# One pool for projections and scan, values moved forward, and a stepwise substitution in an RWKV-7 layer

## The chip, the core and the metric

The kernel runs on one core of a Trainium2 chip. The metric is device time of one execution in microseconds; before the change the median of three runs is 2736.81 us (2734.67 to 2741.68). A core has five engines that matter here: TensorE (PE in the views), VectorE (DVE), ScalarE (ACT), GpSimd (POOL) and SyncE (SP, which issues nearly all transfers). Each has its own instruction order and waits on semaphores of others. DMA moves data between HBM and the core's SBUF.

## The reference, cut to what matters

The reference is a trunk of two layers on 256 tokens with 2048 features. Layer 0 mixes by sparse attention, layer 1 by RWKV-7; each is followed by a squared-ReLU MLP, and all parts are scaled and shifted by products of silu(c). The change touches layer 1's mixer, and in passing the place where silu(c) is made:

```
delta = h_prev - h
xr, xw, xk, xv, xa, xg = (h + delta * mu[i] for i in range(6))
r, k, v = xr @ w_r, xk @ w_k, xv @ w_v
decay = exp(-exp(-softplus(-(w0 + tanh(xw @ w_w1) @ w_w2)) - 0.5))
a = sigmoid(a0 + (xa @ w_a1) @ w_a2)
g = sigmoid(xg @ w_g1) @ w_g2
def step(state, inp):                       # 32 heads of 64, 256 tokens
    sa = einsum('bhij,bhj->bhi', state, -kk_t)
    state = state * w_t + sa * (kk_t * a_t) + v_t * k_t
    return state, einsum('bhij,bhj->bhi', state, r_t)
o = layer_norm(o) * gn_g + gn_b + sum(r * k * r_k) * v
return (o * g) @ w_o
```

## The kernel before, in words

Features lie on the partitions: 16 tiles of 128 features (two heads each) by 256 tokens. All of a weight's products are made with three matmuls in reduced form (`acc3`, L181 to L186: high part of the weight with high and low part of the data, low part with high): a weight comes as four pieces of 128x512, ACT casts the high part (L92) and DVE or POOL subtracts to get the low part (L94). `bufs["g"]` says which of the four pieces' subtractions POOL does.

Layer 1's mixer runs in `rwkv_project` and `rwkv_scan`. The projections go through two loops over the 16 tiles. The first makes r (W_r) and the mixed inputs; xv, the input of the values, is kept. The second, called the W_k loop here, multiplies W_k for tile f and then makes with `elements` all that is elementwise for tile f - 1: the decayed forms of r, k, kk and a, written by ACT to DRAM as `hd`.

The scan turns the recurrence into chunks of 64 tokens, four of them. For each tile `prepare` reads `hd`, makes the value (48 dense matmuls with W_v), the within-chunk matrices `at` (L969), transposes (L975, L980) and a product with v (L994). `inverse` makes the inverses of unit triangular 64x64 matrices: first of the 32x32 diagonal blocks by doubling, four levels of 16 products (L1025) and 16 products (L1032) of 32x32 in each tile, with a masked copy, a transpose by DVE and a copy by ACT between them; then one step from 32 to 64 (L1045, L1052). `chain` then goes through the four chunks one after another: the state's part (L1080), the sum (L1082), the solve (L1085), a copy (L1086), the output (L1088) and the new state (L1099 and after). `finish` normalizes, and `out_group` multiplies with W_o from tile 5 on.

The order on each engine follows a scheduler that takes instructions by priority as their inputs and buffers come free; `high_priority(URGENT)` lets `chain` and `inverse` go ahead of the rest. Three tiles are prepared ahead (AHEAD), two inverses (AHEAD_INV). Projections and scan have SBUF pools of their own, one after the other, beside a third, `keep`, for what lives in both.

## Time and profile before

| | |
|---|---|
| median of three runs | 2736.81 us (2734.67 to 2741.68) |
| profiled execution | 2733.74 us, of which the span is 2732.0 us |
| mean granted clock of TensorE | 0.968 |
| PE busy | 2582.7 us (95%), 21876 matmuls |
| DVE busy | 1863.9 us (68%) |
| ACT busy | 1353.5 us (50%) |
| POOL busy | 1356.4 us (50%) |
| W_k loop | 1342 to 1498 us of the span |
| hand-over to the scan | 1498 to 1567 us |
| scan to the last chain | 1567 to 1947 us |

The span is the time from the first to the last instruction of the profiled execution; the profile is of that one, and the median is over other executions. A matmul of this kernel in full float32 has two records in the trace. Groups in a timeline (xcount) have a start and the time to the end of the last of the group; busy times of neighbouring matmuls overlap, since matmuls are pipelined. The clock column is a share of full speed: TensorE's two levels are 1.2 and 2.4 GHz, and a stretch at the lower one shows as 0.5.

### The profile page before, as it was taken

The page shows a single profiled execution, that of the slowest core. Times are in us where ns is not written, and L with a number is a line of the kernel's source. Part 1 is how long each engine was busy: PE and PEld are TensorE (multiplying, and loading weights), DVE is VectorE, ACT ScalarE, POOL GpSimd, SP SyncE. Part 2 cuts the span into 40 slices and gives each one's busy share as a digit, 9 for nine tenths or more (in the row PEclk, how much of TensorE's full clock was granted, in tenths as well). Part 3 has the DMA queues.
Part 4 walks back from the last instruction along what each step waited for, and adds up shares of the span by engine and source line. Part 5 has one row for each costly group of instructions (what it writes and reads, how often), then busy time and mean ns, then how long its engine had stood idle before and what let it go on. Part 6 is the DMA issues. An engine that isn't in the chain of part 4 may idle for free. (4 is left out here: it accounts for less than half of the span.)

```text
span 2732.0 us, 58247 instructions
## 1 busy us (share of the span) xinstructions
PE 2582.7 (95%) x21876; PEld 2277.7 (83%) x21876; DVE 1863.9 (68%) x2986; ACT 1353.5 (50%) x2964; POOL 1356.4 (50%) x1121
## 2 busy tenths in 40 slices
PE   6898998999999999989889899999789999999997
PEld 3566778988989989879889788888689898898996
DVE  3266568999999999769877557666797244353443
ACT  3334335555554545556555334443445565564553
POOL 1343227568577675755566212232655444444454
PEclk9899999999999999999999889999899999999999
DMA  9997745989999999736476423232486655555553
GB/s 364 402 357 261 266 149 197 322 310 374 322 334 355 324 349 337 267 110 194 141 247 213 157 78 102 93 111 97 168 314 203 212 182 189 192 182 192 186 185 104
DMA packets 263595, 624.33 MB, mean 229 GB/s; under 512 B 29328, under 2 KB 43024, under 8 KB 238352
## 3 DMA queue, kind: packets, MB, share of 16 engines
q1 hardware_dynamic: 256400, 608.03, 64.0%
q10 hardware_dynamic: 6912, 12.59, 1.3%
q8 instruction: 171, 2.80, 0.4%
q14 instruction: 112, 0.92, 0.1%
HBM read 603.72 MB, written 16.78 MB: 227 GB/s over the span
## 5 line engine op out<-in xcount | busy, mean ns | idle before, releaser
L94 POOL TENSOR_TENSOR wlo<-raw,whi 128x512 fp32r<-128x512 f32 x364 | 569.0, 1572 | 535.5 <-ACT whi L92 415.2
L92 ACT CAST whi<-raw 128x512 fp32r<-128x512 f32 x856 | 516.7, 618 | 385.7 <-PE ps_d L185 112.3
L94 DVE TENSOR_TENSOR wlo<-raw,whi 128x512 fp32r<-128x512 f32 x492 | 471.1, 969 | 207.6 <-ACT whi L92 200.1
L94 POOL TENSOR_TENSOR wlo<-more,whi 128x512 fp32r<-128x512 f32 x181 | 278.4, 1541 | 289.9 <-ACT whi L92 209.2
L92 ACT CAST whi<-more 128x512 fp32r<-128x512 f32 x366 | 223.0, 618 | 193.8 <-PE ps_m L418 44.0
L256 DVE CUSTOM_DVE_ANT_0 araw<-araw,cb 128x2048 f32<-128x2048 f32 x112 | 292.2, 2609 | 0.0
L94 DVE TENSOR_TENSOR wlo<-more,whi 128x512 fp32r<-128x512 f32 (+1 forms) x185 | 183.9, 996 | 116.9 <-ACT whi L92 116.3
L184 PE MATMUL ps_d<-A,whi 128*128 128x256 f32 x656 | 195.0, 299 | 12.2 <-ACT B L911 6.9
L185 PE MATMUL ps_d<-A,whi 128*128 128x256 f32 x656 | 189.6, 290 | 4.3 <-DVE A L198 4.2
L186 PE MATMUL ps_d<-A,wlo 128*128 128x256 f32 x656 | 188.4, 288 | 0.3 <-DVE wlo L94 0.3
L401 DVE TENSOR_TENSOR A<-B,A 128x256 fp32r<-128x256 f32 x96 | 101.9, 1061 | 96.1 <-ACT A L400 95.8
L185 PE MATMUL ps_d<-h,whi 128*128 128x258 f32 x560 | 160.7, 287 | 6.1 <-DVE h L377 6.0
L184 PE MATMUL ps_d<-h,whi 128*128 128x258 f32 x560 | 160.4, 286 | 0.0
L186 PE MATMUL ps_d<-h,wlo 128*128 128x258 f32 x560 | 159.2, 284 | 0.0
L184 PE MATMUL ps_m<-h,whi 128*128 128x258 f32 x532 | 151.3, 284 | 0.0
L185 PE MATMUL ps_m<-h,whi 128*128 128x258 f32 x532 | 150.9, 284 | 0.0
L184 PEld LDWEIGHTS ps_d<-A,whi 128*128 128x128 f32 x656 | 127.7, 195 | 27.2 <-ACT B L911 7.7
L186 PE MATMUL ps_m<-h,wlo 128*128 128x258 f32 x532 | 150.0, 282 | 0.0
L397 ACT ACTIVATE B<-B,sm 128x256 f32<-128x256 f32 x128 | 65.1, 508 | 170.6 <-DVE B L396 170.6
L185 PEld LDWEIGHTS ps_d<-A,whi 128*128 128x128 f32 x656 | 127.7, 195 | 8.0 <-DVE A L198 6.8
L186 PEld LDWEIGHTS ps_d<-A,wlo 128*128 128x128 f32 x656 | 127.8, 195 | 1.0 <-issue 0.5
L94 POOL TENSOR_TENSOR xlo<-more,xhi 128x512 fp32r<-128x512 f32 x51 | 103.6, 2031 | 45.5 <-ACT xhi L92 43.9
(545 smaller groups left out, 8200.6 us busy)
## 6 DMA issues: line engine op xcount, KB each, us to landing
araw<-ada_w_in SPq DMA_DIRECT2D x192, 1024.0 KB, 7.1
raw<-mlp_w_in SPq DMA_DIRECT2D x614, 256.0 KB, 4.1
more<-mlp_w_in SPq DMA_DIRECT2D x410, 256.0 KB, 4.5
raw<-b_w_r_in SPq DMA_DIRECT2D x64, 256.0 KB, 3.1
raw<-b_w_k_in SPq DMA_DIRECT2D x64, 256.0 KB, 3.5
raw<-b_w_v_in SPq DMA_DIRECT2D x64, 256.0 KB, 3.6
raw<-b_w_o_in SPq DMA_DIRECT2D x64, 256.0 KB, 3.3
hd<-A ACTq DMA_DIRECT2D x48, 256.0 KB, 4.0
```

Of the source, the lines that this page charges most:

```text
L92: t.nc.scalar.copy(hi[:, :n], r)
L94: e.tensor_tensor(lo[:, :n], r, hi[:, :n].bitcast(F32), op=OP.subtract)
L184: mm(out, wh, m[:, :w], start=i == 0, stop=False)
L185: mm(out, wh, m[:, w:], start=False, stop=False)
L186: mm(out, wl, m[:, :w], start=False, stop=i == n - 1)
L256: nc.vector.tensor_tensor_reduce(out=w, in0=w, in1=s.cb, scale=1.0, scalar=0.0, op0=OP.mult, op1=OP.add, accum_out=acc[:, k:k + 1])
L397: nc.scalar.activation(r, u, AF.Relu, bias=c)
L401: nc.vector.tensor_tensor(t[:, S:], q, t[:, :S].bitcast(F32), op=OP.subtract)
```

## The change

One pool "rwkv" serves projections and scan, and the ring "h" of 16 tiles, free after the projections' inputs are mixed, is used for what lives long (`H`). `value` writes its result to DRAM (`vd`); twelve of the sixteen values are made in the W_k loop, four between the first pair's steps. `within` makes the part of `at` that the inverse needs already in the W_k loop and writes it to DRAM (`nd`). `blocks` inverts all 32x32 blocks of half of the tiles at once on DVE, one matrix on each partition, by 30 steps of a product and a sum, and writes them to DRAM (`xd`): the first half of the tiles in the W_k loop, the second in the scan. `inverse` reads its blocks from there and keeps only the step from 32 to 64. `prepare_pair` and `chain` work on two tiles at a time, with copies and sums of double width. silu(c) is made once, written to DRAM (`cd`) and read where it was made again before. The sums of squares end in three tiles in place of two. (The core of the diff; line numbers in the fences below that are of the changed code differ from those of the code above.)

```diff
-AHEAD, AHEAD_INV = 3, 2
+LAG_N = 3
+LATE_V = 4
+STEPS = 4, 5
...
+    def H(s):
+
+        return s.tp.tile([P, S + 1], F32, name="h", bufs=NF)[:, :S]
...
+        if s.cd is not None:
+            nc.sync.dma_start(s.cb, s.cd[0].partition_broadcast(P))
+            return
+        s.cd = s.dram.tile([1, D], F32, name="cd")
         nc.sync.dma_start(s.cb, s.io["c"].partition_broadcast(P))
         sg = s.tp.tile([P, D], F32, name="araw", bufs=s.bufs["m"])
         nc.scalar.activation(sg, s.cb, AF.Sigmoid)
         nc.vector.tensor_tensor(s.cb, s.cb, sg, op=OP.mult)
+        nc.sync.dma_start(s.cd, s.cb[0:1, :])
...
+        s.bufs["g"] = (1, 2)
+        made, vs, sub = {}, list(range(NF - LATE_V)), None
+        for f in range(NF + LAG_N):
             if f < NF:
                 w = s.wload(io["b_w_k"][f])
                 pk = s.dense(w, xm, cols)
-            if f:
-                s.elements(f - 1, pp, omka, wa0)
-            if f == NF:
-                s.vs[0] = s.value(0, keep.tile([P, S], F32, name="v0"))
+            if 0 < f <= NF:
+                made[f - 1] = s.elements(f - 1, pp, omka, wa0)
+            if vs and (f % 3 or f >= NF):
+                s.value(vs.pop(0), s.H())
+            if f >= LAG_N:
+                s.within(f - LAG_N, *made.pop(f - LAG_N))
+            if f == NF // 2 + LAG_N - 1:
+                sub = s.blocks(0)
+            elif sub:
+                for _ in range(STEPS[0]):
+                    next(sub, None)
             pp = pk
+        assert not vs
+        for _ in sub:
+            pass
+
+    def value(s, f, v, after=None):
+        w = s.wload(s.io["b_w_v"][f])
+        p = s.dense(w, s.xv, [i * P for i in range(16)])
+        if after is not None:
+            s.behind(s.first, after)
+        s.nc.scalar.copy(v, p)
+        s.nc.sync.dma_start(s.vd[f], v)
...
     def rwkv_scan(s):
-        todo, om, pre = [], [], []
-        for f in range(AHEAD):
-            pre.append(s.prepare(f))
-            if not f:
-                s.pairs()
-            if f < AHEAD_INV:
-                s.inverse(f, pre[f])
-        for f in range(NF):
-            cur = pre.pop(0)
+        todo, om = [], []
+        s.pairs()
+        nxt = s.prepare_pair(0)
+        sub = s.blocks(1)
+        for f0 in range(0, NF, 2):
+            cur = nxt
             with s.tc.high_priority(URGENT):
-                s.chain(f, cur)
-            if f + AHEAD_INV < NF:
-                with s.tc.high_priority(URGENT):
-                    s.inverse(f + AHEAD_INV, pre[AHEAD_INV - 1])
-            if f + AHEAD < NF:
-                pre.append(s.prepare(f + AHEAD))
-            om.append(s.finish(f, cur))
...
+                s.chain(f0, cur)
+            if f0 + 2 < NF:
+                nxt = s.prepare_pair(f0 + 2)
+            for i in range(2):
+                f = f0 + i
+                om.append(s.finish(f, cur[i]))
+                for _ in range(STEPS[1] + 1):
+                    next(sub, None)
...
+    def prepare_pair(s, f):
+
+        uv = s.tp.tile([P, 1024], F32, name="big", bufs=3).rearrange("p (i c x) -> p i c x", i=2, c=4)
+        akv, ot = (s.wp.tile([P, 512], F32, name="o", bufs=NO).rearrange("p (i x) -> p i x", i=2) for _ in range(2))
+        out = []
+        for i in range(2):
+            d = s.prepare(f + i, uv[:, i], akv[:, i])
+            d.update(o=ot[:, i], pair=(uv, akv, ot))
+            out.append(d)
+        with s.tc.high_priority(URGENT):
+            for i in range(2):
+                s.inverse(f + i, out[i])
+        if not f:
+            for i in range(2, LATE_V):
+                s.value(NF - LATE_V + i, s.H(), s.last)
+        return out
...
+    def blocks(s, half):
+        nc = s.nc
+        xt = s.tp.tile([P, 1024], F32, name="big", bufs=3).rearrange("p (j i) -> p j i", j=32)
+        for b in range(2):
+            r = slice(b * 32, b * 32 + 32)
+            nc.sync.dma_start(xt[b * 64:b * 64 + 64], s.nd[half].rearrange("p (s t) -> p s t", s=64)[:, r, r])
+        nc.vector.memset(xt.rearrange("p j i -> p (j i)")[:, 0:1024:33], 1.0)
+        for j in range(1, 31):
+            i = 31 - j
+            p = s.H()[:, :j * i].rearrange("p (c i) -> p c i", c=j)
+            o = xt[:, :j, j + 1:]
+            nc.vector.tensor_tensor(p, xt[:, j:j + 1, j + 1:].to_broadcast([P, j, i]),
+                                    xt[:, :j, j:j + 1].to_broadcast([P, j, i]), op=OP.mult)
+            nc.vector.tensor_tensor(o, o, p, op=OP.add)
+            yield
+        nc.sync.dma_start(s.xd[half][0], xt.rearrange("p j i -> p (j i)"))
+        for h in range(2):
+            xn = s.tp.tile([P, 512], F32, name="xv", bufs=NF) if half else s.A()
+            nc.vector.tensor_copy(xn.rearrange("p (i c) -> p i c", c=32), xt.rearrange("p c i -> p i c")[:, h * 16:h * 16 + 16])
+            nc.sync.dma_start(s.xd[half][1][:, h * 512:(h + 1) * 512], xn)
+        yield
...
+    def within(s, f, ar, bk):
+        nc = s.nc
+        pn = s.bank("c")[:, :S]
+        for c in range(4):
+            x = c * P + (0 if c % 2 else 64)
+            for h in range(2):
+                hs = slice(h * 64, h * 64 + 64)
+                nc.tensor.matmul(pn[hs, c * 64:c * 64 + 64], bk[hs, x:x + 64], ar[hs, x:x + 64], start=True, stop=True)
+        n = s.H()
+        nc.vector.tensor_tensor(n.rearrange("p (c t) -> p c t", c=4), pn.rearrange("p (c t) -> p c t", c=4),
+                                s.cv("mask_a")[:, 64:128].unsqueeze(1).to_broadcast([P, 4, 64]), op=OP.mult)
+        for h in range(2):
+            m = f % 8 * 8 + h * 4
+            nc.sync.dma_start(s.nd[f // 8][m:m + 4].rearrange("c (s t) -> s c t", s=64),
+                              n[h * 64:h * 64 + 64].rearrange("p (c t) -> p c t", c=4))
...
-        ar, bk, bp, g = s.A(), s.A(), s.B(), s.B()
-        for t, d in ((ar, s.hd[f][0]), (bk, s.hd[f][1]), (bp, s.hd[f][2][:, :S]), (g, s.hd[f][2][:, S:])):
+        ar, bk, bp, v = s.A(), s.A(), s.H(), s.H()
+        if f < 4:
+            g, bv = s.B(), s.B()
+        else:
+            gb = s.tp.tile([P, 512], F32, name="xv", bufs=NF)
+            g, bv = gb[:, :S], gb[:, S:]
+        for t, d in ((ar, s.hd[f][0]), (bk, s.hd[f][1]), (bp, s.hd[f][2][:, :S]), (g, s.hd[f][2][:, S:]), (v, s.vd[f])):
             nc.sync.dma_start(t, d)
-        v = s.vs.pop(f) if f in s.vs else s.value(f, s.B())
         pb = s.bank("m")[:, :S]
         mm(pb, s.cv("blockones"), bp, start=True, stop=True)
-        bv = s.B()
         nc.vector.tensor_tensor(bv, pb, v, op=OP.mult)
...
+        ph = [s.bank("m") for _ in range(2)]
+        for c in range(4):
+            cc = slice(c * P, c * P + P)
+            for h in range(2):
+                hs = slice(h * 64, h * 64 + 64)
+                last = mm(ph[h][:, cc], bk[hs, cc], ar[hs, cc], start=True, stop=True)
+        if f < 2:
+            s.value(NF - LATE_V + f, s.H(), last)
+        for h, p in enumerate(ph):
...
     def inverse(s, f, d):
         nc = s.nc
         mm = nc.tensor.matmul
-        at, i = d["at"], f % 2
+        at = d["at"]
         rows = [slice(32 * q, 32 * q + 32) for q in range(4)]
         nt = lambda q, u, c0: at[u // 2][rows[q], 2 * (u % 2) + (1 if q < 2 else 0), c0:c0 + 32]
-        z1 = s.z1[i]
-        pair = s.cv("pair").bitcast(U32)
+        zf = s.zf[f % 4]
+        x = s.B(P)
+        def mine(k, q, b):
+            m = b * 64 + f % 8 * 8
+            return s.xd[f // 8][k][m:m + 8].rearrange("(g q) (i c) -> q i g c", q=2, i=32)[q]
         for q in range(4):
-            for h in range(2):
-                src = at[h][rows[q]].rearrange("p (c e) x->p c e x", e=2)[:, :, 1 if q < 2 else 0, 32 * q:32 * q + 32]
-                nc.vector.copy_predicated(z1[rows[q], 2 * h:2 * h + 2, :],
-                                          pair[rows[q]].unsqueeze(1).to_broadcast([32, 2, 32]), src)
+            odd, b = 1 if q < 2 else 0, q % 2
+            nc.sync.dma_start(zf[rows[q], :, b * 32:b * 32 + 32], mine(0, odd, b))
+            if not b:
+                nc.sync.dma_start(x[rows[q]].rearrange("p (u c) -> p u c", u=4), mine(1, odd, b))
         blk = lambda t, q, u: t[rows[q], u * 32:(u + 1) * 32]
...
-        for l in range(4):
-            y = s.yl[i][l]
-            p = s.bank("ij"[i])
-            for u in range(4):
-                for q in range(4):
-                    mm(blk(p, q, u), nt(q, u, 32 * q), blk(x, q, u), start=True, stop=True)
...
-            p = s.bank("ij"[i])
-            for u in range(4):
-                for q in range(4):
-                    mm(blk(p, q, u), blk(y, q, u), blk(z, q, u), start=True, stop=True)
...
+        p = s.bank("i")
...
+        uv, akv, ot = ds[0]["pair"]
+        two = lambda t: t.rearrange("p (i x) -> p i x", i=2)
+            p = s.bank("ab"[f // 2 % 2])
+                rs = [akv[:, i, g] for i in range(2)]
+                one, other = (mm(p[:, i * P:i * P + P], d["ar"][:, cc], st[:, i], start=not i, stop=True,
+                                 skip_group_check=i > 0) for i, d in enumerate(ds))
+                s.behind(other, one)
+                r = s.B().rearrange("p (i x) -> p i x", i=2)
+                nc.vector.tensor_tensor(r[pu], two(p[pu, :S]), akv[pu, :, g], op=OP.add)
+                rs = [r[:, i] for i in range(2)]
+            pd = p[:, S:]
+                for i, d in enumerate(ds):
+                    mm(pd[pu, i * P + h * 64:i * P + h * 64 + 64], d["zf"][pu, 2 * h + c // 2, :], rs[i][pu, hs[h]],
+                       start=True, stop=True)
+            nc.scalar.copy(uv[pu, :, c, :], two(pd[pu]))
+            for i, d in enumerate(ds):
+                for h in range(2):
+                    last = mm(p[pv, i * P + h * 64:i * P + h * 64 + 64], d["at"][h][:, c, xr:xr + 64],
+                              uv[:, i, c, hs[h]], start=st is None, stop=True, skip_group_check=st is not None)
+                pn = two(s.bank("j")[:, :S])
+                for i, d in enumerate(ds):
+                    for h in range(2):
+                        last = s.behind(mm(pn[hs[h], i, hs[h]], d["bkt"][:, c * P + h * 64:c * P + h * 64 + 64],
+                                           uv[:, i, c, hs[h]], start=True, stop=True), last)
+            nc.scalar.copy(ot[pv, :, g], two(p[pv, :S]))
+            if c < 3:
+                pc = s.pc[:, f:f + 2, c:c + 1]
+                new = s.sbd[(f // 2 * 3 + c) % 3]
+                for h in range(2):
+                    o, i = new[hs[h], :, hs[h]], pn[hs[h], :, hs[h]]
+                    if st is None:
+                        nc.vector.tensor_tensor(o, i, pc[hs[h]].to_broadcast([64, 2, 64]), op=OP.mult)
+                    else:
+                        nc.vector.tensor_tensor(o, i, st[hs[h], :, hs[h]], op=OP.add)
+                    nc.vector.tensor_tensor(new, new, pc.to_broadcast([P, 2, P]), op=OP.mult)
...
-        with tc.tile_pool(name="keep", bufs=1, reuse_waits="tile") as keep:
-            with t.phase("project", a=21, b=16, l=3, m=0):
-                t.rwkv_project(keep)
-            with t.phase("scan", a=23, b=13, m=0, g=(1, 2)):
-                t.rwkv_scan()
-                t.ada(1000)
+        t.pc = t.fix.tile([P, NF, 4], F32, name="pc")
+        with t.phase("rwkv", a=21, b=11, l=2, m=0):
+            t.rwkv_project()
+            t.rwkv_scan()
+            t.ada(1000)
```

How PE's order stands at the hand-over (xv is the values' input, wlo and whi the parts of W_v, hd is read into A and B). Before, first the projection's last dense matmul, then tile 0 and the first level of its inverse:

```order
L186 MATMUL ps_d<-xv,wlo 128x256
L958 MATMUL ps_m<-B,cst 128x256
L969 MATMUL ps_m<-A 128x128 x8
L975 MATMUL ps_m<-cst,A 128x128 x4
L980 MATMUL ps_m<-cst,v_18436 128x128 x2
L1025 MATMUL ps_i<-xz_18607,A 32x32 x12
L994 MATMUL ps_m<-A 64x64 x2
L1025 MATMUL ps_i<-xz_18607,A 32x32 x4
L994 MATMUL ps_m<-A 64x64 x6
L1032 MATMUL ps_i<-z_0_18571,y_0_18573 32x32 x16
L184 MATMUL ps_d<-xv,whi 128x256
```

After, the last matmuls of the W_k loop are those of `within` (L1015), and tile 0's products (L1046) are followed by dense ones:

```order
L192 MATMUL ps_d<-xv,whi 128x256
L193 MATMUL ps_d<-xv,wlo 128x256
L1015 MATMUL ps_b<-A 64x64 x8
L316 MATMUL ps_j<-cst,sm 64x128 x4
L1015 MATMUL ps_a<-A 64x64 x8
L1036 MATMUL ps_m<-h,cst 128x256
L1046 MATMUL ps_m<-A 128x128 x8
L189 MATMUL ps_d<-xv,whi 128x256
L192 MATMUL ps_d<-xv,whi 128x256
```

The levels L1025 and L1032 are gone from there, and a whole value of 48 dense matmuls stands between L1046 and the next steps of tile 0.

How PE's order stands in the scan before tile 5. Before, one tile's chain (L1080) between levels of the inverses (L1025, L1032) and dense matmuls of values:

```order
L1080 MATMUL ps_a<-sbd_18565,A 128x128
L1025 MATMUL ps_i<-xz_20877,A 32x32 x4
L994 MATMUL ps_m<-A 64x64 x8
L186 MATMUL ps_d<-xv,wlo 128x256
L184 MATMUL ps_d<-xv,whi 128x256
L185 MATMUL ps_d<-xv,whi 128x256
L186 MATMUL ps_d<-xv,wlo 128x256
L184 MATMUL ps_d<-xv,whi 128x256
L185 MATMUL ps_d<-xv,whi 128x256
L186 MATMUL ps_d<-xv,wlo 128x256
L184 MATMUL ps_d<-xv,whi 128x256
L1032 MATMUL ps_j<-xz_20598,y_1_18589 32x32 x7
```

After, the chain of pair 0 (L1138 state, L1147 solve, L1152 output, L1158 new state) between the steps of the next pair (L1036, L1046, L1055, L1060, L1073):

```order
L1158 MATMUL ps_j<-big,A 64x64 x4
L1036 MATMUL ps_m<-h,cst 128x256
L1046 MATMUL ps_m<-A 128x128 x4
L1138 MATMUL ps_a<-lo,A 128x128 x2
L1046 MATMUL ps_m<-A 128x128 x4
L1147 MATMUL ps_a<-B,lo 64x64 x4
L1152 MATMUL ps_a<-big,A 64x64 x4
L1158 MATMUL ps_j<-big,A 64x64 x4
L1055 MATMUL ps_m<-cst,A 128x128 x4
L1138 MATMUL ps_a<-lo,A 128x128 x2
L1060 MATMUL ps_m<-cst,h 128x128 x2
L1147 MATMUL ps_a<-B,lo 64x64 x4
```

The chain's steps carry twice the matmuls, and no dense matmul stands between them there.

How SP's order stands at the hand-over. Before, the loads of tile 0 (L955) behind weights of values:

```order
L877 DMA B<-rd_13910 128x256
L167 DMA raw<-b_w_v_in 128x512 x13
L955 DMA A<-hd_0_13911 128x512
L955 DMA A<-hd_0_13912 128x512
L955 DMA B<-hd_0_13913 128x256 x2
L167 DMA raw<-b_w_v_in 128x512 x2
L955 DMA A<-hd_1_13914 128x512
```

After, the last writes of `within` (nd) and of the substituted blocks (xd, from the tile big) ahead of the loads of tile 0 (L1034) and of the blocks (L1092):

```order
L172 DMA raw<-b_w_v_in 128x512 x3
L855 DMA vd_13974<-h 128x256
L1021 DMA nd_13958<-h 64x4x64 x4
L927 DMA xd_13959<-big 128x1024
L931 DMA xd_13960<-A 128x512
L1034 DMA A<-hd_0_13909 128x512
L1034 DMA A<-hd_0_13910 128x512
L1034 DMA h<-hd_0_13911 128x256
L1034 DMA h<-vd_13963 128x256
L1092 DMA lo<-xd_13959 32x4x32 x8
L1034 DMA B<-hd_1_13914 128x256
L1092 DMA lo<-xd_13959 32x4x32 x8
```

The loads of tile 0 stand now behind transfers that wait for DVE's results.

## Rows read from the trace of the kernel before

**Rows 1.** The page, section 1: busy time, share of the span, instructions.

```profile
PE 2582.7 (95%) x21876; PEld 2277.7 (83%) x21876; DVE 1863.9 (68%) x2986; ACT 1353.5 (50%) x2964; POOL 1356.4 (50%) x1121
```

**Rows 2.** Windows: us; busy PE, PEld, DVE, ACT, POOL; clock; DMA share; GB/s.

```profile
1342.00:1498.00 156.00, 141.22 (x1120) 133.89 (x1119) 124.83 (x236) 87.45 (x204) 93.07 (x162) 0.95 0.63 207
1498.00:1567.00 69.00, 58.84 (x829) 52.52 (x828) 38.60 (x89) 23.70 (x60) 23.41 (x26) 0.83 0.46 152
1567.00:1947.00 380.00, 374.36 (x6736) 322.08 (x6735) 253.42 (x712) 160.92 (x442) 109.57 (x96) 0.97 0.31 100
```

**Rows 3.** Windows of 20 us, the first and the last of 1520 to 1620.

```profile
1520.00:1540.00 20.00, 12.21 (x119) 10.04 (x120) 5.23 (x15) 4.43 (x15) 1.35 (x2) 0.53 0.48 169
...
1600.00:1620.00 20.00, 19.97 (x276) 16.63 (x277) 10.80 (x35) 7.17 (x22) 2.29 (x3) 0.67 0.09 28
```

**Rows 4.** Windows, of L1025 alone and then of L1032 alone: PE and PEld busy.

```profile
1520.00:1920.00 400.00, 40.35 (x2048) 28.72 (x2048) 0.94 0.31 101
1520.00:1920.00 400.00, 36.93 (x2048) 27.01 (x2048) 0.94 0.31 101
```

**Rows 5.** Lines of PE, 1500 to 1960: busy us, mean ns, idle before.

```profile
L969 PE MATMUL ps_m<-A 64*128 64x128 f32 x256 | 40.7, 311 | 0.0
L994 PE MATMUL ps_m<-A 64*64 64x64 f32 x256 | 15.4, 234 | 0.0
L958 PE MATMUL ps_m<-B,cst 128*128 128x256 f32 x32 | 11.3, 437 | 8.4 <-DMA B<-hd 8.4
```

**Rows 6.** Timeline of PE: start, us, line and operation, count.

```profile
1541.97 0.45 PE L1025 MATMUL ps_i<-xz,A 32*32 32x32 f32 x32
1542.36 1.16 PE L969 MATMUL ps_m<-A 64*128 64x128 f32 x8
...
1543.67 0.28 PE L184 MATMUL ps_d<-xv,whi 128*128 128x256 f32 x1
...
1544.74 0.28 PE L184 MATMUL ps_d<-xv,whi 128*128 128x256 f32 x1
1544.95 0.71 PE L969 MATMUL ps_m<-A 64*128 64x128 f32 x4
```

**Rows 7.** Waits of PE, 1342 to 1520: total us, times, longest us.

```profile
PE ps_d L184 <- ACT B L911: 6.9, 4, 3.4
PE ps_d L185 <- DVE A L198: 3.7, 8, 1.2
PE ps_j L304 <- POOL sm L922: 1.9, 3, 1.3
```

**Rows 8.** Lines of DVE and POOL, 1380 to 1520.

```profile
L94 DVE TENSOR_TENSOR wlo<-raw,whi 128x512 fp32r<-128x512 f32 x55 | 42.9, 785 | 7.5 <-ACT whi L92 7.3
L918 DVE TENSOR_TENSOR B<-B 128x256 f32<-128x256 f32 x14 | 6.3, 452 | 0.2
L94 POOL TENSOR_TENSOR wlo<-raw,whi 128x512 fp32r<-128x512 f32 x7 | 9.8, 1416 | 2.8 <-ACT whi L92 2.0 <-PE ps_j L304 0.8
```

**Rows 9.** Timeline of PE, last chunk; in brackets the wait before.

```profile
1945.00 0.46 PE L1080 MATMUL ps_b<-sbd,A 128*128 128x128 f32 x2 [0.83 <-DVE sbd L1106]
1945.84 0.44 PE L1085 MATMUL ps_b<-rs,zf 64*64 64x64 f32 x4 [0.38 <-DVE rs L1082]
1946.63 0.44 PE L1088 MATMUL ps_b<-A 128*64 128x64 f32 x4 [0.35 <-ACT A L1086]
1951.06 0.69 PE L1128 MATMUL ps_m<-cst,fin 128*128 128x128 f32 x2 [3.98 <-DVE fin L1125]
```

**Rows 10.** SP's queue, two issues; then DMA groups: KB each, us to landing.

```profile
1944.90 0.33 SPq L167 DMA_DIRECT2D raw<-mlp_w_in  x1
1945.28 0.42 SPq L206 DMA_DIRECT2D cb<-c_in  x1
...
raw<-b_w_k_in SPq DMA_DIRECT2D x64, 256.0 KB, 3.5
B<-rd SPq DMA_DIRECT2D x16, 128.0 KB, 3.1
```

More of the change, by code (lines that the diff above doesn't have):

```diff
@@ L37 @@
 LG = 4
-FIN, OM = 6, 4
 ADA_INDEX, ADA_TOPK, ADA_HEAD, ADA_OUT = 2, 6, 2, 3
@@ L183, in acc3 @@
             w = m.shape[-1] // 2
-            mm(out, wh, m[:, :w], start=i == 0, stop=False)
+            one = mm(out, wh, m[:, :w], start=i == 0, stop=False)
+            if i == 0:
+                s.first = one
             mm(out, wh, m[:, w:], start=False, stop=False)
@@ L1038, in inverse @@
-        for q in range(4):
-            o = 32 * (q % 2)
-            (nc.scalar.copy if q % 2 else nc.vector.tensor_copy)(zf[rows[q], :, o:o + 32], p[rows[q], :P].rearrange("p (u x)->p u x", u=4))
-        p = s.bank("ij"[i])
+        p = s.bank("i")
         for u in range(4):
```

154 lines of the change are left out of this document (43 added, 111 removed).

## The prediction, made blind

> **What bounds the kernel now.** Read the engine line of the page first: PE is busy for 95% of the span [rows 1], so only work taken from PE, or gaps of PE, can be worth anything. Next come the windows of the stages that the change touches [rows 2]. The reader is to see three of them: the W_k loop, the hand-over to the scan, and the scan up to the last chain. In the scan PE is busy 374.36 of 380 us with 6736 matmuls at a granted clock of 0.97; DVE stands at 253.42 us there. In the W_k loop PE is busy 141.22 of 156 us, DVE 124.83, POOL 93.07. The hand-over has 58.84 of 69 us at 0.83. So the scan is PE's own work, and the two stages before it lose some 25 us to gaps. The windows of 20 us [rows 3] show where: 12.21 busy us of the first 20 with a clock of 0.53 (nearer to 1.2 than to 2.4 GHz), which is the stretch after PE waited 8.4 us for the first load of hd [rows 5]; and 0.67 where the first chains run, with PE busy throughout.
>
> **What the change removes.** The doubling levels, L1025 and L1032, have 2048 records each and are 40.35 and 36.93 us busy [rows 4]: 77 us if each record had PE alone. They don't: the timeline has 32 of them (0.45 us as a group) with the next matmul, of L969, 0.39 us after the group's start [rows 6]. 4096 records are 128 such groups; 128 x 0.39 = 50 us. The order splits many groups into ones that alternate with other work, so I take 54, near the lower end, with 50 and 77 as bounds. **-54.** That work stands in stages where PE is nearly always busy [rows 2], so it comes off the end. Its copies, transposes and masks on DVE and ACT go with it, beside PE's work, and count nothing.
>
> **What it adds on PE.** `within` has 8 matmuls of 64x64 for each of 16 tiles: 128, the number that L994 has, whose row shows 256 records (two passes each) and 15.4 us busy [rows 5]. Busy times overlap; the dense matmuls are each busy 0.28 us but start 0.12 us apart (nine of them from 1543.67 to 1544.74 [rows 6]), so that less than half of the busy time may remain: 6 to 15.4. I take **+12**, near the row.
>
> **What it moves.** (a) Twelve of the sixteen values go into the W_k loop and four into the first pair's steps; their matmuls are the same. In the scan's order the places where dense matmuls give way to small ones go from about 155 to 80. One such change costs about 0.15 us: from L969's group, 1542.36 + 1.16 = 1543.52, to L184's start 1543.67 [rows 6]. 75 x 0.15 = **-11**. The way in, from L184 at 1544.74 to L969 at 1544.95, is 0.21 against the dense 0.12; with that 0.09 on top it is -18: bounds 0 and -18.
> (b) In the W_k loop PE waited for ACT, DVE and POOL some 6.9 + 3.7 + 1.9 us in the largest three of its waits [rows 7]. With a value's 48 dense matmuls (48 x 0.12 = 5.8 us) behind most waits, PE has something else in its queue, if the weights are there. **-10** of these 12.5, bounds 0 and -15 (the small waits too), and +19 (half as much again as the 12.5) where the other engines become late. Do they? The loop grows from 156 us to about 227 (12 values of 5.8 us, `within` 12, less the waits). DVE has now 124.83 us. Half of its subtractions L94 go to POOL: the W_k half, 32 x 0.785 = -25; the values' half, 24 x 0.785 = +19. Added are the masks of `within`, 16 x 0.45 = 7, and the first half of the substitution: 60 TENSOR_TENSORs of 30 to 240 elements in a partition, at most the 452 ns of 128x256 [rows 8], so 27 us. 153 in all. POOL gets 56 subtractions of 1416 ns [rows 8]: 93 + 79 = 172. Both stay below 227, so PE stays the bound, though with less room than before.
> (c) SP issues more in the loop: per iteration 4 + 3 weight loads and 3.75 of rd, vd and nd. One issue costs 0.33 to 0.42 us [rows 10], so 11 cost 4.5 us of 14. What hides it is that loads run ahead; a load that waits for its ring's buffer holds the vd and nd writes behind it, and a write that waits for DVE holds the loads. The price of lost cover is a landing, 3.5 us [rows 10], for one iteration.
> (d) The hand-over. Before, PE stood waiting for B<-hd [rows 5]. Now the order puts the last writes of nd and of the substituted blocks (xd) ahead of A<-hd_0 on SP: they wait for the last DVE steps, which come behind the last tile's elements. Then pair 0 needs five loads and its 16-KB pieces of xd. The gap stays, of about the size that it has, and the first pair's steps have four values between them, as the first tiles' steps had before. **0**, bounds -15 (no gap, clock back) and +8 (the gap doubles).
> (e) Chains of two tiles. A chunk's steps alone stand at 1945.00 (L1080), 1945.84 (L1085) and 1946.63 (L1088, 0.44 long), after 0.83 us of waiting for the state [rows 9]: 0.83 + 0.84 + 0.79 + 0.44 = 2.9 us, and some 0.3 for the state's own matmuls, 3.2. For two tiles the copies and sums are twice as wide, the matmuls double: I take 4.5 to 5.5 us a chunk, 18 to 22 for a pair. PE's own work for pairs 1 and 2 (with no dense matmuls before tile 5) is 13 to 16 us: a tile's share of L969 and L994, (40.7 + 15.4) / 16 = 3.5 [rows 5], and 3 to 4.5 for its chain's matmuls, whose groups of 0.44 to 0.46 [rows 9] overlap when they stand close; from pair 3 on W_o fills the waits. The chain of pair 0 has the four values only in part. So 5 to 6 us for each of two pairs: **+12**, bounds 0 and +35.
> (f) silu of c and the third square tile: the second activation and product over 128x2048, on ACT and DVE, fall out; the sums of squares at the end wait for other work. PE waits there for `fin` (3.98 us before L1128 [rows 9]), and the MLP behind is PE's. **0**, bounds -4 (that wait gone) and +1 (two issues of cd and a third square).
>
> At (d) a rule bears on the small reads. The rows show 0.33 us for an issue and 3.1 and 3.5 us from issue to landing for 128 and 256 KB [rows 10]; issues ten times closer than landings. The Trainium skill, "DMA: Bandwidth & Descriptors", section "Rules for kernel authors", says that below 64 KB one pays mostly overhead, and its section "Bandwidth" has a fixed cost of about 2.0 us for a DMA. By the rows pair 0's 12 reads cost 12 x 0.33 = 4 us of issue plus one landing; by an estimate from that page, one after another, 24 us, and the sum would be some 20 us worse. No row here shows 16-KB reads.
>
> **The sum.** -54 + 12 - 11 - 10 + 0 + 12 + 0 = -51 us. The profiled execution took 2733.74 us, 1.74 beside its span of 2732.0; the changed one comes to a span of 2681.0 and 2682.7 us. The median of the runs shown, 2736.81, lies 3.07 above the profiled one: 2685.8, so **2686 us**.
>
> **Rivals.**
> 1. *The pairs' chains bind for longer.* A chunk of 6.5 us instead of 5: a pair 26, and three pairs (0 to 2) lack 12 each, 36 instead of 12: -27, 2710 us. For: hops of 0.35 to 0.83 us are waiting alone [rows 9], and PE's queue holds matmuls behind a waiting one. Against: two tiles share each hop. Chance 0.18.
> 2. *The hand-over, the switches and the clock give back more.* -54 + 12 - 18 - 15 - 12 + 0 = -87, 2650 us. For: 0.53 and 0.67 of clock [rows 3] are worth 12.21 x 0.47 = 6 and 19.97 x 0.33 = 7 us if they rise to 1. Against: the small matmuls that stood there leave, and nothing dense replaces them before tile 5. Chance 0.22.
> 3. *Slower: SP's queue in the W_k loop.* Weight loads stand behind writes that wait for elements and blocks, and PE waits for weights. The gain of 51 is used up from 51 / 16 = 3.2 us lost in an iteration, about one landing of 3.5 [rows 10]; at 5 us it is +80 - 51 = +29, 2766 us. For: the DMA share is already 0.63 in that loop [rows 2], and the ring of lora weights shrinks from 3 buffers to 2. Against: 112 loads of W_k and W_v in 227 us leave 2 us for each, six times its issue. Chance 0.10.
> 4. *The small reads come one after another.* With a landing of 3.1 us each [rows 10], 12 reads take 37 us instead of 5, and only pair 0 has nothing to cover it: +32, so -19, 2718 us. The Trainium skill's rule on small transfers, cited above, speaks for it. Chance 0.06.
> 5. *The change gives nothing that can be measured*: several of these bounds at once, within 8 us of before. Chance 0.04.
>
> The forecast has the remaining 0.40. 0.3% of this time is 8 us, about what a measurement can tell from no change. Faster: 0.40 + 0.18 + 0.22 + 0.06 = 0.86; within: 0.04; slower: 0.10. The range takes in cases 1, 2 and 4 with some of their spread and leaves out 3 and 5 (0.14) and a rest of case 2: 2640 to 2722 us.
>
> **What would show it.** The windows after must show about 4100 fewer 32x32 records, the W_k loop at some 225 us with PE above 95% busy, and the scan near 300. In the W_k loop, waits of PE for a DMA of weights would be rival 3. At the hand-over, the row of the first L1036 shows the gap (8.4 before); a wait of L1100 or L1107 for xd would be rival 4. In the scan, waits of L1138 and L1147 before tile 5 that add up to 12 us are the forecast, 36 rival 1; a granted clock of 1.0 throughout is rival 2. It is wrong at its root if DVE or POOL is busy for over 95% of the loop, or if the levels' departure takes less than 45 us from PE's path.

## The result: 1.6% slower, and the profile after

The changed kernel took 2780.12 us (median of 4 runs, 2774.96 to 2788.68) against 2737.26 of the kernel before, measured beside it (median of 4): a ratio of 1.0156, 95% interval 1.0137 to 1.0174. The forecast was 2686, in a range of 2640 to 2722. The profiled execution of the changed kernel took 2774.96 us, 1.76 beside its span of 2773.2; it is the fastest of the four, 5.2 below their median.

The page's engine line after, as in [rows 1]: 3824 matmul records are gone, and PE is busy 20.4 us less in a span that is 41.2 us longer.

```profile
PE 2562.3 (92%) x18052; PEld 2269.2 (82%) x18052; DVE 1814.5 (65%) x2697; ACT 1317.9 (48%) x2807; POOL 1384.4 (50%) x1151
```

The windows after, with the columns of [rows 2]: the first MLP, the W_k loop, the scan from the first L1036 to the last chain, and the stretch from there to the last MLP's sums. Then three of the same stages of the kernel before, cut at the same events.

```profile
581.50:1151.50 570.00, 560.51 (x3482) 506.26 (x3481) 543.05 (x480) 299.69 (x605) 374.62 (x201) 0.99 0.93 329
1363.00:1628.60 265.60, 235.08 (x1985) 222.82 (x1984) 194.78 (x323) 124.28 (x275) 173.72 (x230) 0.93 0.65 195
1637.60:1975.40 337.80, 301.66 (x2797) 262.06 (x2797) 173.48 (x405) 115.85 (x273) 81.44 (x75) 0.81 0.36 104
1975.40:2038.50 63.10, 34.75 (x220) 31.43 (x220) 50.46 (x71) 25.90 (x61) 41.59 (x60) 0.78 0.51 176
```

```profile
576.40:1133.20 556.80, 556.11 (x3484) 504.63 (x3483) 544.70 (x483) 298.58 (x605) 393.79 (x201) 1.00 0.94 337
1342.70:1519.20 176.50, 161.72 (x1296) 153.31 (x1295) 141.37 (x266) 96.34 (x224) 109.79 (x182) 0.96 0.64 207
1526.50:1947.10 420.60, 412.03 (x7380) 354.47 (x7380) 273.70 (x768) 172.79 (x471) 113.41 (x99) 0.95 0.31 99
```

Read them as a balance. The starts of the first MLP show +5.1 ahead of it; the first MLP has +13.2, the stretch to the W_k loop +2.0, the W_k loop +89.1, the gap at the hand-over +1.7 (9.0 against 7.3), the scan -82.8, the way to the last MLP +13.6 (63.1 against 49.5), the rest -0.6: 41.2 together. The +5.1 is not shown to be the change's: over the 20 kernels of this document the first MLP starts at 575.8 to 586.6 us, also in those that change nothing ahead of the scan (e5: 581.7), and 576.4 is almost the earliest. Nine values of 48 matmuls went from the scan to the loop (3 stood there before, 12 now): 432 x 0.12 = 52 us. So the loop's 89.1 are 52 moved, 12 to 15 of `within`, and some 23 lost; the scan should have lost 52 and 54, and lost 83. Its granted clock tells more than its busy share: 0.81, where it was 0.95.

The shape of that in the scan, against [rows 3]: stretches of 20 us in which PE is busy for four fifths, at a mean clock of 0.59 and 0.51, near the lower level of 1.2 GHz.

```profile
1700.00:1720.00 20.00, 16.05 (x160) 12.78 (x160) 9.92 (x36) 6.54 (x17) 4.87 (x6) 0.59 0.24 57
...
1740.00:1760.00 20.00, 15.93 (x105) 13.70 (x105) 13.51 (x40) 4.40 (x12) 4.09 (x5) 0.51 0.09 27
```

PE's waits in the W_k loop and at the hand-over, 1363 to 1640, against [rows 7] and L958 in [rows 5]: those on ACT and DVE are still there, that on POOL has more than doubled, and the 9.0 us of the first load of hd answer to 7.3 (the 8.4 of [rows 5] are two waits, of which the hand-over has 7.3).

```profile
PE ps_m L1036 <- DMA h<-hd: 9.0, 1, 9.0
PE ps_j L316 <- POOL sm L983: 4.5, 5, 2.3
PE ps_b L189 <- ACT h L960: 3.7, 2, 2.7
PE ps_d L189 <- ACT h L854: 3.5, 2, 2.0
PE ps_d L192 <- DVE A L205: 3.3, 2, 1.8
```

### The profile page after: what moved, and what is told of

Its sections match the earlier page's. It is cut to its first block, busy times and chain, and to the rows that moved or that the text cites. A ratio compares the mean times of both kernels' runs of the same rounds, so it can differ in the third digit from the quotient of the medians.

```text
span 2773.2 us, 50349 instructions
## 1 busy us (share of the span) xinstructions
PE 2562.3 (92%) x18052; PEld 2269.2 (82%) x18052; DVE 1814.5 (65%) x2697; ACT 1317.9 (48%) x2807; POOL 1384.4 (50%) x1151
## 5 line engine op out<-in xcount | busy, mean ns | idle before, releaser
L95 POOL TENSOR_TENSOR wlo<-raw,whi 128x512 fp32r<-128x512 f32 x398 | 624.5, 1578 | 587.7 <-ACT whi L93 523.0
L95 DVE TENSOR_TENSOR wlo<-raw,whi 128x512 fp32r<-128x512 f32 x458 | 459.8, 1015 | 222.1 <-ACT whi L93 212.8
L268 DVE CUSTOM_DVE_ANT_0 araw<-araw,cb 128x2048 f32<-128x2048 f32 x112 | 285.4, 2550 | 0.0
L414 DVE TENSOR_TENSOR A<-B,A 128x256 fp32r<-128x256 f32 x96 | 112.4, 1171 | 95.6 <-ACT A L413 95.3
L189 PE MATMUL ps_d<-h,whi 128*128 128x258 f32 x560 | 160.5, 287 | 11.4 <-ACT whi L93 11.4
L189 PE MATMUL ps_d<-xv,whi 128*128 128x256 f32 x512 | 158.0, 314 | 10.1 <-ACT xv L204 9.1
L192 PE MATMUL ps_d<-xv,whi 128*128 128x256 f32 x512 | 155.7, 304 | 1.9 <-DVE xv L205 1.8
L193 PE MATMUL ps_d<-xv,wlo 128*128 128x256 f32 x512 | 154.1, 301 | 0.0
L189 PEld LDWEIGHTS ps_d<-A,whi 128*128 128x128 f32 x656 | 129.6, 199 | 23.1 <-issue 5.2
```

Source lines behind the costliest of these rows:

```text
L95: e.tensor_tensor(lo[:, :n], r, hi[:, :n].bitcast(F32), op=OP.subtract)
L189: one = mm(out, wh, m[:, :w], start=i == 0, stop=False)
L192: mm(out, wh, m[:, w:], start=False, stop=False)
L193: mm(out, wl, m[:, :w], start=False, stop=i == n - 1)
L268: nc.vector.tensor_tensor_reduce(out=w, in0=w, in1=s.cb, scale=1.0, scalar=0.0, op0=OP.mult, op1=OP.add, accum_out=acc[:, k:k + 1])
L414: nc.vector.tensor_tensor(t[:, S:], q, t[:, :S].bitcast(F32), op=OP.subtract)
```

## The experiments

Below, "scan" is the stretch from the first L958 or its successor to the last matmul of the chain in the profiled execution, "way out" the stretch from there to the last MLP's sums. A hop is a step of the chain for whose result the next step waits. Totals are medians; a stage is read from one execution, so that a few us in a stage tell nothing by themselves.

**The two edits at the MLPs.** ACT's timeline of the changed kernel behind the last chain (columns as in [rows 9]) shows the square of x's 15th tile waiting for the last W_o group, in front of all that the MLP needs from ACT:

```profile
2005.81 0.42 ACT L324 ACTIVATE sq<-x 128x256 f32<-128x256 f32 x1 [11.51 <-DVE x L470]
```

e1 goes back to two tiles:

```diff
-        k = f - NF + 3
-        q = s.sq[max(k, 0)] if f == 0 or k > 0 else s.B()
+        k = 0 if f == 0 else 2 if f == NF - 1 else -1
+        q = s.sq[k] if k >= 0 else s.B()
```

> The sums of squares end in two tiles again, as before the change; all else is the changed kernel. Theory A (ACT's order): at the entry of the last MLP the square of the 15th tile has a buffer of its own, stands early in ACT's order and waits 11.5 us for the last W_o group with all of the MLP's activations and casts behind it. Then the stretch from the last chain to the MLP's first sums (63 us in the changed kernel, 49 before) falls by 5 to 13 us, and the total by as much. Rival B (SBUF of the one pool is released late): the stretch stays within 3 us of 63, since the activations would have waited for their tiles anyway.

2773.62 us. The way out fell from 63.1 to 59.4 only, and the scan grew from 337.7 to 347.6. The stretch from the first MLP's first matmul to the projections, of which neither theory spoke, fell from 636.0 to 624.3 (621.0 before). Theory A has less than the least that it claimed; most of the way out's loss stays without a shown cause.

e2 makes silu(c) three times again (the early return through `cd` is taken out of `spread_c`):

> silu(c) is made three times again, as before the change; all else is the changed kernel. Theory A: the first MLP, 13 us longer in the changed kernel (570 against 557), lost them because the product and the activation that went from its start let DVE's order start with other work, so that PE waited 9.5 us for low parts of weights; the first MLP comes back to within 3 us of 557 and the total falls by 8 to 15 us. Rival B (the ring of 11 tiles in place of 12 costs the MLP its time): the first MLP stays at 565 or more.

2774.13 us. From the first MLP to the projections it took 620.0 us (621.0 before, 636.0 changed): theory A. Its first MLP has PE busy throughout again:

```profile
584.30:1140.00 555.70, 555.46 (x3483) 504.70 (x3482) 542.46 (x481) 299.38 (x604) 383.09 (x201) 1.00 0.95 337
```

But the total gained 6, not 15, and the scan took 345.2. e8 undoes both edits:

> The changed kernel with silu(c) made three times and the sums of squares in two tiles, as before the change. The orders of PE, DVE and ACT up to the end of the first MLP are then those of the kernel before. Theory A (what the changed kernel lost ahead of the recurrence, 5 and 15 us, are these two edits): the first MLP starts at 576 to 579 and the stretch to the projections is 621 as before; total 18 to 26 us less than the changed kernel. Rival B (the two do the same thing, so that one of them alone gives all): total as with one of them, 2774.

2776.44 us, with 620.9 from the first MLP to the projections and a scan of 357.8. The first stretch and the total speak for rival B: either edit undone alone gives 11.7 (e1) or 16.0 us (e2) of that stretch's 15 back, both together 15.1, and the total is that of one alone. What the first MLP wins, the scan loses, and neither theory had that. PE's order in the scan hardly differs (in some 40 places of 1430 groups), and time times granted clock, an estimate of its work at full clock, hardly either: 337.8 x 0.81 = 274 in the changed kernel, 357.9 x 0.75 = 268 in e8, 268 and 269 in e1 and e2. So the longer scans have a lower clock and not more work. Why the clock is lower in them was not found, and with one execution of each the spread has a part in it.

**The levels, cut alone in the kernel before.** e5 leaves one level of four, e13 none (`range(1)`, `range(0)` in the loop of L1025 and L1032).

> The kernel before with one doubling level in place of four in each inverse: 3072 records of 32x32 leave (it leaves out three quarters of the doubling). Nothing else of the change is in it. Theory A (the forecast's term): 96 groups of 0.39 to 0.42 us leave PE's path, 38 to 40 us less. Rival B (the small products filled PE while the chain waited, and held the granted clock up): the scan gets shorter by under 25 us and its granted clock falls from 0.97 to below 0.92.

> The kernel before with no doubling level (all four left out, nothing in their place); no steps on DVE, no reads of blocks. Theory A (a floor: with the last level the filler goes): the scan stays at 376 or more, 381.8 with one level, so that the fourth level gives under 6 us. Rival B (no floor, it was the steps and the reads): 368 or less, the fourth level gives its 13.

e5: 2703.02 us against 2738.28, ratio 0.9859 (0.9833 to 0.9885); e13: 2688.30 against 2742.64, 0.9799 (0.9775 to 0.9823). Their scans, in this order:

```profile
1533.60:1915.40 381.80, 370.84 (x4291) 321.07 (x4291) 245.95 (x669) 164.78 (x437) 112.88 (x98) 0.93 0.36 104
```

```profile
1534.30:1895.00 360.70, 347.10 (x3255) 298.99 (x3255) 247.72 (x634) 161.78 (x421) 112.11 (x97) 0.96 0.38 110
```

Their scans are 38.8 and 59.9 us shorter than the scan before, their totals 35.3 and 54.3: the forecast's -54 holds, and there is no floor under it at 376. The last level alone gave 21 of the scan, more than rival B of e13 said. The clock is 0.93 and 0.96 without the small products, so they did not hold it up.

**The buffers.** e6 gives the kernel before the rings of the one pool (`b=11, l=2` for `b=16, l=3`).

> The kernel before with the projections' pool at 11 working tiles (16) and 2 lora buffers (3), as the one pool has them. Theory A (the rings are what the W_k loop of the changed kernel lost): the W_k loop grows from 177 us by 10 us or more with waits for lora weights. Rival B (what was added to the loop lost it): it grows by less than 4 us.

2735.36 us, ratio 0.9984 (0.9968 to 1.0000), W_k loop 176.0 for 176.5: rival B. Fewer buffers in the projections cost nothing by themselves.

**The values, moved alone.** In the kernel before:

```diff
+        s.bufs["g"] = (1, 2)
+            if vs and (f % 3 or f >= NF):
+                k = vs.pop(0)
+                nc.sync.dma_start(s.vd[k], s.value(k, s.B()))
```

> The kernel before with twelve values made in the W_k loop and written to DRAM, half of the loop's subtractions on POOL, nothing else of the change: nine values of 5.8 us change places, 52 us. Theory A (the loop has no room, and there the changed kernel lost 35 us): the W_k loop grows by 65 us or more, the scan shrinks by 40 to 55, total 8 to 25 us more than before. Rival B (the forecast: the values fill the waits of the loop): it grows by 35 to 48, total 5 to 25 us less.

2798.70 us against 2738.89, ratio 1.0207 (1.0179 to 1.0235): worse than the whole change. W_k loop and scan, and the loop's first wait of PE:

```profile
1355.20:1599.50 244.30, 217.74 (x1729) 208.16 (x1727) 170.50 (x249) 119.00 (x270) 170.01 (x229) 0.95 0.60 196
1611.10:2016.10 405.00, 389.24 (x6948) 326.68 (x6948) 256.41 (x750) 148.16 (x424) 86.99 (x81) 0.85 0.26 81
```

```profile
PE ps_j L304 <- POOL sm L926: 14.4, 11, 2.3
```

The loop grew by 67.8 for 52 us of matmuls. Its waits say why: PE waits 14.4 us for POOL, which has half of the subtractions now, where it was 1.9, while the wait for ACT fell from 6.9 [rows 7] to 0.6, as the forecast hoped. (The values without POOL's subtractions were not tried.) The scan, relieved of the same 52, gave back 15.6; with the gap at the hand-over (11.6 for 7.3) the three are +56.5 of the +59.8. Time times granted clock says where the rest is: 420.6 x 0.95 = 400 before, 405.0 x 0.85 = 344 now. By this estimate the work fell by 56 at full clock, and the time hardly: without the dense matmuls between the chain's, PE runs the rest at a lower clock. Theory A is right on the loop; scan and total lie outside both theories. The Trainium skill, "TensorE: Matmul & The Clock Gate", section "HAM oscillation — how this bites in real kernels", tells of a kernel whose waits for DMA between its groups of matmuls let the clock fall each time anew. The trace agrees on the clock, with 0.85 for 0.95, and not on the waits: behind its first load this scan has PE waiting for results of DVE and ACT, 2.0 us at the longest.

e4 takes four values back out of the loop, into the steps of pair 1 of the changed kernel (`LATE_V = 8`).

> Eight values in the scan in place of four: four between pair 0's steps and four between pair 1's; the W_k loop makes eight. Theory A (the granted clock): the scan's stretch between 1700 and 1800, PE busy 85% at 0.77, has dense matmuls to fill it again; the scan gets longer by less than the 23 us that the W_k loop loses: total 8 to 20 us less. Rival B (PE's work is what counts wherever it stands): total within 5 us of the changed kernel.

2795.97 us, slower still: the loop gave 14.9 and the scan took 30.2. Both theories fall; the scan's clock is 0.82 for 0.81. 192 matmuls for 30 us are 0.157 each, or 7.5 us a value, where one that left the scan of the kernel before gave 1.7 (15.6 / 9, from e10). There the values stand one by one between the hops, here four together in one pair's steps. That this makes the difference is argued and not tried: e4 has chains of two tiles as well. In the loop, too, the price differs: 3.7 us a value (14.9 / 4) here, 7.5 (67.8 / 9) in e10.

e7 puts filler there instead, three matmuls on constants behind each chunk's products:

```diff
+            pf = s.bank("d")
+            for _ in range(3):
+                last = s.behind(mm(pf[:, :S], s.ident, s.cst[:, :S], start=True, stop=True), last)
```

> The changed kernel with three matmuls of 128x256 in float32 on constants behind each chunk of the chain, whose result nobody reads: 96, about 42 us of PE work at the full clock. Theory A (the scan loses by the granted clock, 0.81 on the mean, because PE pauses): the scan's clock rises above 0.9, and the scan grows by less than 15 us or gets shorter. Rival B (PE's work counts wherever it stands, at whatever clock): the scan grows by 35 us or more and the clock stays.

2803.54 us, 23 more. The scan's row:

```profile
1646.80:1988.50 341.70, 306.19 (x2791) 258.83 (x2791) 157.64 (x377) 106.80 (x257) 73.19 (x68) 0.88 0.32 92
```

Only 4 us longer at 0.88 for 0.81, but the way out grew by 16.7, as 193 matmuls of W_o slipped behind the chain. About half of the filler's 42 us was free. The clock rose as theory A says, if not above 0.9; the price lies between the two theories.

**The substitution, alone in the kernel before**, and with pieces of it moved. e3 is the changed kernel without the steps; e9 adds `within`, `blocks` and the short `inverse` to the kernel before; e14 is e9 without the steps in the scan; e15 has these on POOL, e16 all of them, e17 those of the changed kernel.

> Leaves out the 30 steps of the stepwise substitution in both halves; reads, writes and copies of the blocks stay. Theory A (DVE late at the end of the W_k loop): the stretch from 1600 to the first product of pair 0, where PE is busy 21 of 38 us, loses 6 to 12 us, and the W_k loop's clock there comes back; total 8 to 18 us less. Rival B (SP's transfers and PE's own gaps set it): less than 4 us.

> The kernel before with the substitution alone: within, blocks and the short inverse of the change, in the old pools (12 working tiles and 2 lora buffers in the projections, to make room) and the old order of values and single-tile chains. Theory A (the forecast's terms for the levels and for within hold): -52 for four levels by the 38.7 that three gave, +12 to 15 for within: total 30 to 45 us less than before, the scan 50 us shorter, the W_k loop 12 to 20 longer. Rival B (the substitution's DVE steps, its writes and 16-KB reads cost the W_k loop and the hand-over 35 us): W_k loop and gap 30 us or more longer, total within 12 us of before.

> The substitution alone, without its 30 steps in the scan (the second half of the blocks stays as it was read; reads and writes remain). Theory A (DVE's steps stand between the chain's sums on DVE's queue): the scan falls from 406.8 by 15 us or more. Rival B (they lie beside it): by less than 6.

> The substitution alone (e9) with the scan's 30 steps on POOL, which is busy for 110 of the scan's 407 us; the first half stays on DVE. Theory A (DVE's queue is the cost): the scan comes from 406.8 to 378 to 390, near the 377.6 without steps; total 2718 to 2732, faster than before. Rival B (the steps cost by their results coming late, or POOL's work slows DVE's): scan 400 or more, total 2745 or more.

> As e15, and the W_k loop's 30 steps on POOL too, where POOL does fewer subtractions in this version. Theory A: as e15 or up to 6 us better, since DVE is the busier one in the loop. Rival B (POOL's steps take twice DVE's time and end late): the gap at the hand-over grows by 5 us or more.

> The changed kernel with the scan's steps on POOL. Theory A: the scan falls from 337.7 towards the 325 that it has without steps; total 8 to 15 us less than the changed kernel. Rival B: within 5 us of it.

e3: 2762.17 us, W_k loop -8.0, gap -2.2, scan -12.5; the end of the loop gave what theory A said, and the scan, of which neither spoke, as much again. e9: 2750.24, ratio 1.0043 (1.0025 to 1.0061), rival B by its total and by neither in its place: the loop has +13.8, which is `within` with the first half's steps, but the scan only -13.7. e14: 2718.13, ratio 0.9907, scan 377.6: theory A by its size, the steps cost the scan 29.2. e15: 2747.79, scan 410.5: on POOL they cost as much, so DVE's queue is not the cause, and theory A falls. e16: 2761.24, 13 more than e15, with 12 of it in the loop and the gap unchanged (12.2); e17: 2788.71, scan 344.0, 9 more than the changed kernel. In both neither theory holds. The scans of e9, e14 and e15:

```profile
1552.40:1959.20 406.80, 370.68 (x3255) 318.95 (x3255) 215.55 (x521) 152.22 (x389) 109.62 (x97) 0.88 0.36 105
```

```profile
1553.00:1930.60 377.60, 359.52 (x3267) 309.46 (x3267) 201.23 (x464) 151.53 (x389) 109.67 (x98) 0.93 0.40 113
```

```profile
1549.30:1959.80 410.50, 366.52 (x3267) 317.14 (x3268) 203.96 (x464) 151.16 (x390) 142.58 (x158) 0.87 0.37 104
```

DVE has the same 201 to 204 us in the second and third; what they don't share, beside POOL's time, is the 30 tiles that the steps take from the ring of `prepare`. e18 gives the steps two tiles of their own, and PE's order in the scan becomes that of e14 in more than nine tenths of its rows (e9 has about half of them):

```diff
-            p = s.B()[:, :j * i].rearrange("p (c i) -> p c i", c=j)
+            p = s.tp.tile([P, S], F32, name="st", bufs=2)[:, :j * i].rearrange("p (c i) -> p c i", c=j)
```

> The substitution alone (e9), all steps on DVE, with a ring of two tiles of their own for the steps' products. PE's order in the scan is then nearly that of the version without steps. Theory A (the steps cost by the tiles they take from prepare's ring): the scan falls from 406.8 to 376 to 385, near the 377.6 without steps; total 2715 to 2727, 10 to 22 us less than before. Rival B (the steps cost by their time on an engine, or by results that come late): scan 398 or more, total 2742 or more.

2724.35 us against 2741.03, ratio 0.9939 (0.9924 to 0.9954): theory A, and a kernel that beats both. Its scan, then 40 us from 120 us into the scan, in e9 and in e18:

```profile
1557.20:1939.70 382.50, 360.93 (x3267) 310.05 (x3267) 221.18 (x524) 151.99 (x389) 109.44 (x98) 0.92 0.39 112
```

```profile
1672.40:1712.40 40.00, 29.73 (x263) 24.02 (x263) 22.51 (x65) 13.17 (x38) 7.74 (x8) 0.73 0.32 94
1677.20:1717.20 40.00, 38.82 (x354) 31.93 (x353) 21.88 (x48) 15.46 (x43) 9.76 (x9) 0.94 0.35 100
```

The ring's other user shows the delay: `prepare` of tile 8 starts 190 us into the scan in e9, 158 in e18 and 152 in e14. The steps' results come earlier in e18, too (their last write starts at 1726.3 us for 1753.8), but PE waits as long for the reads of xd in both (8.4 and 8.2 us), so that this is not what was won. The 17 us by which e14's scan stands above that of e13 (377.6 and 360.7) were not taken apart.

**Parts together.** e11 joins e9 and e10; e12 joins e9 with chains of two tiles.

> Both together: substitution and twelve values in the W_k loop, in the old pools, with single-tile chains, silu(c) three times and two square tiles. What separates it from the changed kernel is the one pool, the chains of two tiles, and the two edits at the MLPs. Theory A (parts add up): total is before plus the sum of the two parts alone, within 8 us. Rival B (values and substitution share DVE, POOL and SP in the loop): 15 us or more above that sum.

> Substitution and chains of two tiles, in the old two pools (18 large and 12 small working tiles in the scan), with the values made one by one through the scan as before, silu(c) and squares as before. Theory A (the chain's latency is the floor under the scan once the small products leave; two tiles at a time halve its hops, and the values spread through the scan fill the rest): the scan falls from 406.8 with the substitution alone to 355 to 375; total 2700 to 2722, faster than before. Rival B (the forecast's view, chains of two tiles cost 12 where nothing fills them): scan 400 or more, total 2745 or more.

e11: 2790.90 us, +52.0, where the parts give 59.8 + 11.4 = 71.2: 19 below the sum, so neither. Its scan of 378.4 stands against 337.7 in the changed kernel and 357.8 in e8, which has silu(c) and the squares as e11 has them: -40.7 or -20.6 for chains of two tiles, the one pool and the other place of the last four values together. Here, too, it is clock: 378.4 x 0.73 = 276 for 274 and 268. e12: 2756.03, scan 413.5: rival B's figures, but it had 18 large and 12 small tiles for the scan, and the steps took of the latter; what the chains alone are worth stays open.

## Why the prediction was wrong, step by step

- **The levels, -54, and `within`, +12:** right in size. All four levels are -54.3 in the total and -59.9 in the scan (e13), three -35.3 and -38.8 (e5). The loop of e9 has +13.8 for `within` and the first half's steps together; `within` alone was not run.
- **(a) and (b), the values, -11 and -10:** the step that failed. "Their matmuls are the same" is true of the matmuls and not of their price: e10 has +59.8 for the move, with POOL's subtractions, alone. In the scan before, they cost 1.7 us each, between the chain's hops; in the loop 7.5 (67.8 / 9). The sum has them at 5.8 in either place, and its bounds allowed for +19 in the loop and nothing in the scan. The sign that the prediction named, a loop of some 225 us with PE above 95% busy, failed as well: 265.6 us, 89%.
- **(a), the 0.15 us of a change from small to dense matmuls,** is read to the second dense matmul. In the timeline of [rows 6] a row between the two that it used holds the first, which starts before L969's group ends at 1543.52, so this price has no row under it:

```profile
1543.44 0.39 PE L186 MATMUL ps_d<-xv,wlo 128*128 128x256 f32 x1
```

- **The clock of the scan** has no term in the sum; rival 2 has it as a gain alone. It fell from 0.95 to 0.81. At 0.95 the scan's 274 (337.8 x 0.81) would be 288 us, an estimate; the forecast's terms give 420.6 - 52 - 54 - 11 + 12 = 316, and 338 were measured.
- **(b), the sums of DVE and POOL:** each below the loop's length, as said, and of no use: PE waited for single results of them nonetheless. POOL's 172 us were met (173.72) in part by luck, since the sum starts from 93.07 in a window that leaves out the loop's last 20 us (109.79 in all); DVE's 153 were 194.78.
- **The substitution's steps** are in the sum as 27 us of DVE in the loop (28.3 measured); their second half, in the scan, has no term. Its DVE time there (24 us in e9) is not what costs, as e15 confirms. Not counted was that the steps take tiles of `prepare`'s ring: the steps cost 29.2 us in the scan of e9, of which e18 gives back 24.3. In the changed kernel they take tiles of the ring "h"; e3 has 12.5 for its scan, and whether that is the ring too was not tried.
- **(d), the hand-over, 0, and rival 4:** right and rejected. The gap is 9.0 for 7.3 us, and PE waits for xd at L1100, the sign of rival 4, once for 1.6 us. SP's 16-KB reads land in 1.7 to 2.8 us while their issues stand 0.46 apart (8 in 3.70 us), against 3.1 and 3.5 us for 128 and 256 KB [rows 10]:

```profile
lo<-xd SPq DMA_DIRECT2D x64, 16.0 KB, 1.7
B<-xd SPq DMA_DIRECT2D x32, 16.0 KB, 2.8
```

The Trainium skill's fixed cost of a DMA, about 2.0 us, is of that size; it stands in "DMA: Bandwidth & Descriptors" under "Anatomy of one DMA — SWDGE (gpsimd) path", for DMAs that GpSimd issues, and not under "Bandwidth". That the reads follow each other four to six times closer than they land is what keeps it from adding up.

- **(e), chains of two tiles, +12:** open. The sign named for it were waits at L1138 and L1147 of 12 us, 36 for rival 1; PE has 11.7 us of them in the whole scan, so rival 1 is rejected. Against single-tile chains in a scan without the dense matmuls (e11), pairs with the one pool and the values' place are 21 to 41 us shorter.
- **(f), silu and the squares, 0:** +15 in the first MLP, which either edit undone gives back for the most part (e1, e2, e8), and 3.7 of the 13.6 on the way out (e1). In the total, undoing both gives 3.7 us only, as the scan takes the rest. Bounds of -4 and +1 were too narrow: an edit that takes an operation away from the start of a stage can move what the scheduler places behind it.
- **Rival 3, the slower side,** had the right place, the W_k loop, and the wrong mechanism: PE waited there for POOL, ACT and DVE. The lora weights stand one link behind: ACT waited for them 24.8 us in the loop, 14.6 before. The smaller ring alone costs nothing (e6).

Of the difference of 92 us between forecast and measured spans (2681.0 and 2773.2), the W_k loop has 35 (+89 for +54), the scan 22 (-83 for -105), the stretches ahead of the projections 20, the way out 14. Shown are the price of moving the values (e10), the first MLP's loss (e1, e2, e8) and the steps' tiles (e18), the second in the changed kernel and the others in the kernel before; how the 22 us of the scan divide between values, steps and chains in the changed kernel is not.

## What to carry to other kernels

Matmuls that stood one by one between the hops of a dependent chain gave back less than a third of their time when they left, so ask what a stage loses with its filler, and price a move at both places. A helper that takes tiles from a shared ring costs what the ring's other users then do later; give it tiles of its own before moving it to another engine. In a scheduled program, compare the stages that an edit was priced at nothing for, too: here the first MLP and the way out hold 27 of the 92 us. Multiply a stage's time by its granted clock before saying that its work grew.

## What the runs showed of the hardware

TensorE's granted clock fell where the dense matmuls between the chain's steps were gone: 0.85 for 0.95 over a whole scan when nine values left it (e10), and it rose from 0.81 to 0.88 when matmuls that compute nothing came in (e7). PE's busy share does not tell it alone: in the changed kernel's scan two stretches of 20 us with 16.05 and 15.93 us busy had 0.59 and 0.51, a third with 16.45 (1780 to 1800) had 0.88. The small products did not matter for it: with all of them gone and the values in place the clock was 0.96 (e13).
